# An mLSTM norm without its divisions, a gate maximum taken per tile, and a convolution tap on ScalarE, in a one-core decoder layer

## The chip, the cores and the metric

The kernel runs on one core of one Trainium2 chip. The metric is the device time of one execution in microseconds; the time before is the median of three runs. Engines are named as the profile names them: PE (TensorE matmul), PEld (its weight load), DVE (VectorE), ACT (ScalarE), POOL (GpSimd), SP (SyncE, which here only issues DMAs).

## What is computed

One decoder layer over 1024 tokens of width 1024, in float32. The reference, cut to the parts that the change touches:

```
h = rms_norm(x);  proj = h @ w_in;  u, vm, z, ipre, fpre, qa, ka, va = split(proj)
c = silu(causal_short_conv(u, conv_w, conv_b))            # 4 taps, per channel
# mLSTM, 4 heads x 128, chunks of 128 tokens, running-max stabiliser
b   = cumsum(log_sigmoid(fpre));   g = b_last - b + logi
m_new = maximum(b_last + m, max(g))                       # carried from chunk to chunk
...
den = sum(s) + inter_w * (q . n_prev)
hm  = num / maximum(abs(den), exp(-m_t))
hm  = rms_norm(hm, mh_norm_g) + skip_m * c;   ym = sigmoid(z) * hm
# beside it: dilated attention, 8 heads x 64 -> ya
x = x + concat(ym, ya) @ w_out
# PEER: per token 8 x 16 of 16384 single-neuron experts
x = x + sum_k gelu(h2 . expert_u[idx_k]) * gate_k * expert_v[idx_k]
```

## The kernel before

The 1024 tokens are eight tiles of 128, in three groups: tiles 0-1, 2-5 and 6-7. For each group in turn the program projects (`channels_in`, `project_gates`, `project_conv`, `project_values`, `project_attention`), runs attention with the mLSTM heads woven in (one mLSTM head-half after every fourth attention step, every second one in the last group), then `queries`: the output projection (`acco`, L564), the residual (L567), the second norm, the query projection (`accq`, L598) and the search for the 16 best keys.

The experts are evaluated in two ways. Tiles 2-5 (the middle group, `DENSE`) go through `dense_experts` (L741): all 16384 experts, as matmuls `pu` (up) and `pv` (down), 3072 of each, in pieces of eight chunks; the gates for them are spread out by one-hot products `pg` (`spread_gates`, L710, with casts and copies on ACT), stored to DRAM as `gate_d`, and read back as `gg`. The buffers of `da` (L762) let nine chunks of `pu` stand before a `gg` is needed. Tiles 0, 1, 6 and 7 go the sparse way: POOL gathers 128 rows of 1024 numbers per indirect DMA (L801, five buffers `gt`), and a consumer takes each: for the up side a DVE product with a sum (L813, 128 per tile), for the down side of tiles 0 and 1 a matmul `pov` (L844, two gathers and four matmuls per step, with a small DVE instruction L836 ahead), for the down side of tiles 6 and 7 a DVE multiply-add (L858).

Nobody writes the order of the instructions by hand: a scheduler simulates the program's time line and writes each engine's list from it. Each engine then works through its list in that order. Sparse work, dense work and the front are mixed in the lists, so a changed instruction can change the place of all that comes after it.

The places that the change touches. `gates` (L355) works on 4 partitions (the heads) and n tiles of tokens: after the cumulative sum `bc` (L368) and `gi = logi - bc` (L369) it takes, tile after tile, a running maximum (a scan, L372) that starts from the state `mst`, and then the next state (L373). `mlstm` ends with the norm: L457 and L458 make the denominator, L459 its reciprocal, L460 and L461 its square times the sum of squares, `rstd` (L159 on DVE, the power -1/2 on POOL at L161), L463 the product of both factors, and L465 scales the head (`hn`); PE then transposes it (`pth`, L468), and DVE adds skip and gate (L471, L472) into `mix`, which `queries` needs. `project_conv` copies the accumulator to `uh` on ACT (L267), writes three carried columns (L266), and applies the first tap with the bias (L270) and three further taps (L273) on DVE.

Of the kernel before, what the change touches and what calls it, by code (L numbers as in the profile page):

```python
# [20 lines left out]
P = 128  # L21
# [22 lines left out]
def hybrid_layer(ctx, tc, x, g1, w_in, w_if, conv_w, conv_b, wq, wk, if_b, mh_g, skip, qn_g, kn_g,  # L44
# [212 lines left out]
    def project_conv(g, th, tl):  # L257

        n = GROUPS[g][1]
        W = n * P  # L260
        with pool("su") as st:
            for blk in range(2):
                accs = by_channel(stream(w_in, blk, th, tl, n, True, "u"), n)
                for h, a in enumerate(accs, 2 * blk):
                    uh = st.tile([P, 3 + W], F32, name="uh", bufs=2)
                    nc.vector.tensor_copy(uh[:, 0:3], halo[:, h])  # L266
                    nc.scalar.copy(uh[:, 3:], a)  # L267
                    nc.vector.tensor_copy(halo[:, h], uh[:, W:W + 3])
                    y = st.tile([P, W], F32, name="cy", bufs=2)
                    nc.vector.tensor_scalar(y, uh[:, 0:W], cw_s[:, h, 0:1], cb_s[:, h:h + 1],  # L270
                                            op0=ALU.mult, op1=ALU.add)
                    for j in range(1, 4):
                        nc.vector.scalar_tensor_tensor(y, uh[:, j:j + W], cw_s[:, h, j:j + 1], y,  # L273
                                                       op0=ALU.mult, op1=ALU.add)
                    nc.scalar.activation(uh[:, 0:W], y, AF.Sigmoid)
                    nc.vector.tensor_tensor(y, y, uh[:, 0:W], op=ALU.mult)
                    c_d[g, h] = dram.tile([P, W], F32, name=f"c{g}{h}")
                    nc.sync.dma_start(c_d[g, h], y)
# [76 lines left out]
    def gates(g, cl, ml, gi, gf):  # L355

        tile0, n = GROUPS[g]
        full = [MH, n, P]
        mr = cl.tile(full, F32, name="mr", bufs=2)
        ab = ml.tile([MH, n * P], F32, name="ab", tag="w2r", bufs=2)  # L360
        nc.vector.scalar_tensor_tensor(ab, gf, -1.0, gf, op0=ALU.mult, op1=ALU.max)
        nc.scalar.activation(ab, ab, AF.Exp, scale=-1.0)
        nc.scalar.activation(ab, ab, AF.Ln, bias=1.0)
        nc.vector.scalar_tensor_tensor(gf, gf, 0.0, ab, op0=ALU.min, op1=ALU.subtract)
        bc = ml.tile(full, F32, name="bc")
        for c in range(n):
            f = gf[:, c * P:(c + 1) * P]
            nc.vector.tensor_tensor_scan(bc[:, c], f, f, 0.0, op0=ALU.add, op1=ALU.bypass)  # L368
        nc.vector.tensor_tensor(gi, gi, bc, op=ALU.subtract)  # L369
        for c in range(n):  # L370
            t = tile0 + c
            nc.vector.tensor_tensor_scan(mr[:, c], gi[:, c], gi[:, c], mst[:, t:t + 1], op0=ALU.max, op1=ALU.max)  # L372
            nc.vector.tensor_tensor(mst[:, t + 1:t + 2], mr[:, c, P - 1:P], bc[:, c, P - 1:P], op=ALU.add)  # L373
        pc = pst.tile([P, 4, n, MH], F32, name="pc", tag="tp")
        for q in range(4):
            row = gi
            if q:
                row = ml.tile(full, F32, name="row", tag="w2r", bufs=2)
            if q == 1:
                nc.vector.tensor_tensor(row, mst[:, tile0:tile0 + n, None].to_broadcast(full), mr,  # L380
                                        op=ALU.subtract)
            elif q == 2:
                nc.vector.scalar_tensor_tensor(row, bc, -1.0, mr, op0=ALU.mult, op1=ALU.subtract)
            elif q == 3:
                nc.vector.tensor_tensor(row, gi, mr[:, :, P - 1:P].to_broadcast(full), op=ALU.subtract)
            for c in range(n):
                nc.tensor.transpose(pc[:, q, c], row[:, c], ident[0:MH, 0:MH])
        wcol = cl.tile([P, n, MH], F32, name="wcol", bufs=2)
        nc.vector.tensor_copy(wcol, pc[:, 0])
        ecol = cl.tile([P, 3, n, MH], F32, name="ecol", bufs=2)  # L390
        nc.scalar.activation(ecol, pc[:, 1:4], AF.Exp)
        pa = pst.tile([P, n, MH], F32, name="pa", tag="tp")
        nc.tensor.matmul(pa, lastsel, ecol[:, 0], start=True, stop=True)
        acol = cl.tile([P, n, MH], F32, name="acol", bufs=2)
        nc.vector.tensor_copy(acol, pa)
        return mr, wcol, ecol, acol

    def mlstm(g, half, h, ml, cols, mix):
# [57 lines left out]
        dn = num[:, :, P]  # L456
        nc.vector.scalar_tensor_tensor(sm[:, 1], dn, -1.0, dn, op0=ALU.mult, op1=ALU.max)  # L457
        nc.vector.tensor_tensor(sm[:, 1], sm[:, 1], ecol[:, 1, :, h], op=ALU.max)  # L458
        nc.vector.reciprocal(sm[:, 2], sm[:, 1])  # L459
        nc.vector.tensor_tensor(sm[:, 3], sm[:, 2], sm[:, 2], op=ALU.mult)  # L460
        nc.vector.tensor_tensor(sm[:, 3], sm[:, 3], sm[:, 0], op=ALU.mult)  # L461
        r = rstd(sm[:, 3], P, HT, ml, "rm")
        nc.vector.tensor_tensor(sm[:, 4], r, sm[:, 2], op=ALU.mult)  # L463
        hn = ml.tile([P, HT, P], F32, name="hn", tag="w2m", bufs=5 if g == 0 else 6)
        nc.vector.tensor_tensor(hn, num[:, :, 0:P], sm[:, 4, :, None].to_broadcast([P, HT, P]), op=ALU.mult)  # L465
        pt = pml.tile([P, HW], F32, name="pth", tag="ml")
# [561 lines left out]
```

## Time and profile before

| what | value |
|---|---|
| median of 3 runs | 3063.17 us (3061.2 to 3078.7) |
| profiled execution, its own time | 3072.45 us |
| its span | 3070.7 us |
| PE busy | 2752.9 us (90%) |
| DVE busy | 2355.9 us (77%) |
| ACT busy | 1231.2 us (40%) |
| POOL busy | 1423.7 us (46%) |
| DMA moved | 891.52 MB, mean 290 GB/s |

Busy is the time in which an engine had an instruction in work. Shares over the whole span mix stages: in the first 1680 us the layer's projections, attention and key search stand beside the sparse gathers of tiles 0 and 1; from there to the end PE does the dense experts while the gathers of tiles 6 and 7 run beside it. The rows below are taken stage by stage for that reason.

### The profile page before, as it was taken

To read this page: it belongs to the slowest core of one execution; us is meant where nothing else is said; L and a number is where in the kernel's file an instruction comes from. 1 tells how busy PE (TensorE), PEld (TensorE's weight loads), DVE (VectorE), ACT (ScalarE), POOL (GpSimd) and SP (SyncE) were. 2 spreads that over 40 slices of the span, in tenths; PEclk is the share of its full clock that TensorE was granted. 3 is DMA by queue.
4 is the path that set the end of the run, shared out by engine and by line. 5 is a ranking of instruction groups with operands and counts; after the bars stand their busy time and mean duration, and the time that the engine had idled before them with its cause. 6 is when DMAs were issued, how large, how long until landed. Compare 5 with 4: busy or idle time off the path is not lost.

```text
span 3070.7 us, 43024 instructions
## 1 busy us (share of the span) xinstructions
PE 2752.9 (90%) x14382; PEld 2174.1 (71%) x14382; DVE 2355.9 (77%) x5611; ACT 1231.2 (40%) x2271; POOL 1423.7 (46%) x1139
## 2 busy tenths in 40 slices
PE   6978757798849999889888999999999999999999
PEld 5868557576637565567655887887888787888787
DVE  4559887679874697758874888888998888898853
ACT  4643323354413323589985222332332232333222
POOL 0100567447673444544553455455555555555510
PEclk9979878587869998899998999999999999999999
DMA  6644789789898898798889999999999999999952
GB/s 196 182 149 125 263 296 338 267 317 312 311 334 294 288 322 291 235 330 297 316 298 310 321 335 319 317 335 327 335 329 356 335 315 336 338 337 317 334 181 76
DMA packets 370900, 891.52 MB, mean 290 GB/s; under 512 B 34120, under 2 KB 135496, under 8 KB 366581
## 3 DMA queue, kind: packets, MB, share of 16 engines
q0 software_dynamic: 147456, 536.94, 49.4%
q1 hardware_dynamic: 209076, 307.78, 30.6%
q10 hardware_dynamic: 14144, 44.05, 3.8%
q8 instruction: 113, 1.85, 0.2%
q14 instruction: 111, 0.90, 0.1%
HBM read 831.97 MB, written 61.38 MB: 291 GB/s over the span
## 4 chain that ended last, share of the span: by engine, by line
PE 31%; DMA 7%; issue 7%; DVE 6%; POOL 4%; ACT 2%; POOLq 0%; DVEq 0%; SPq 0%; ACTq 0%
DMA gg<-gate_d 5%; PE pu L154 5%; PE pu L153 5%; PE pu L155 5%; PE pv L154 5%; PE pv L155 5%; PE pv L153 5%; POOL gt L801 4%; DVE hot L722 1%; PE pg L737 1%; DMA gt<-in_expert_u_dram,idx 1%; ACT gs L738 1%; DMA vr<-in_expert_v_dram 1%; PE pov L844 1%; DVE gt L813 1%
## 5 line engine op out<-in xcount | busy, mean ns | idle before, releaser
L801 POOL DMA_INDIRECT gt<-in_expert_u_dram,idx x512 | 679.0, 1326 | 629.3 <-DVE gt L813 370.8
L813 DVE SCALAR_TENSOR_TENSOR gt<-gt,h2s 128x1024 f32<-128x1024 f32 x512 | 617.5, 1219 | 79.5 <-DMA gt<-in_expert_u_dram,idx 78.8
L801 POOL DMA_INDIRECT gt<-in_expert_v_dram,idx x256 | 342.2, 1337 | 281.5 <-DVE acc L858 237.3
L154 PE MATMUL pv<-vlo,dah 128*128 128x512 f32 x1024 | 402.8, 394 | 14.2 <-DVE vlo L790 14.2
L801 POOL DMA_INDIRECT gt<-in_expert_v_dram,idxt x256 | 270.1, 1055 | 310.6 <-PE pov L844 247.8
L153 PE MATMUL pu<-h2th,uhi 128*128 128x512 f32 x1024 | 406.4, 397 | 1.2 <-ACT da L763 1.2
L155 PE MATMUL pu<-h2th,ulo 128*128 128x512 f32 x1024 | 406.3, 397 | 0.7 <-DVE ulo L758 0.7
L154 PE MATMUL pu<-h2tl,uhi 128*128 128x512 f32 x1024 | 406.5, 397 | 0.0
L155 PE MATMUL pv<-vhi,dal 128*128 128x512 f32 x1024 | 401.0, 392 | 0.0
L788 ACT CAST vhi<-vr 128x512 fp32r<-128x512 f32 x256 | 158.2, 621 | 459.2 <-PE pv L155 411.8
L858 DVE SCALAR_TENSOR_TENSOR acc<-gt,act,acc 128x1024 f32<-128x1024 f32 x256 | 327.8, 1281 | 16.3 <-DMA gt<-in_expert_v_dram,idx 14.0
L153 PE MATMUL pv<-vhi,dah 128*128 128x512 f32 x1024 | 317.6, 394 | 13.9 <-ACT dah L149 11.9
L168 ACT CAST wh<-wr 128x512 fp32r<-128x512 f32 x291 | 178.6, 621 | 292.2 <-DMA wr<-in_w_in_dram 54.8
L170 DVE TENSOR_TENSOR wl<-wr,wh 128x512 fp32r<-128x512 f32 x291 | 199.4, 691 | 79.0 <-ACT wh L168 71.3
L154 PEld LDWEIGHTS pv<-vlo,dah 128*128 128x128 f32 x1024 | 193.3, 189 | 61.2 <-DVE vlo L790 19.1
L153 PEld LDWEIGHTS pv<-vhi,dah 128*128 128x128 f32 x1024 | 193.3, 189 | 59.3 <-ACT dah L149 12.3
L790 DVE TENSOR_TENSOR vlo<-vr,vhi 128x512 fp32r<-128x512 f32 x256 | 175.2, 686 | 76.5 <-ACT vhi L788 74.4
L756 ACT CAST uhi<-ur 128x1024 fp32r<-128x1024 f32 x128 | 134.5, 1051 | 235.7 <-PE pu L154 228.1
L153 PEld LDWEIGHTS pu<-h2th,uhi 128*128 128x128 f32 x1024 | 192.7, 188 | 49.8 <-issue 1.7
L154 PEld LDWEIGHTS pu<-h2tl,uhi 128*128 128x128 f32 x1024 | 192.8, 188 | 47.6 <-issue 2.5
L155 PEld LDWEIGHTS pu<-h2th,ulo 128*128 128x128 f32 x1024 | 192.8, 188 | 46.8 <-DVE ulo L758 1.3
L155 PEld LDWEIGHTS pv<-vhi,dal 128*128 128x128 f32 x1024 | 193.6, 189 | 42.1
(280 smaller groups left out, 5727.2 us busy)
## 6 DMA issues: line engine op xcount, KB each, us to landing
ur<-in_expert_ut_dram SPq DMA_DIRECT2D x128, 512.0 KB
vr<-in_expert_v_dram SPq DMA_DIRECT2D x256, 256.0 KB
wr<-in_w_in_dram SPq DMA_DIRECT2D x144, 256.0 KB
gate_d<-gs ACTq DMA_DIRECT2D x32, 1024.0 KB
gg<-gate_d SPq DMA_DIRECT2D x16, 2048.0 KB
wr<-in_w_query_dram SPq DMA_DIRECT2D x96, 256.0 KB
wr<-in_w_out_dram SPq DMA_DIRECT2D x48, 256.0 KB
gt<-in_expert_u_dram,idx POOLq DMA_INDIRECT x512
```

The costliest lines, as they stand in the source:

```text
L153: nc.tensor.matmul(ps, lh, rh, start=first, stop=False)
L154: nc.tensor.matmul(ps, lh, rl, start=False, stop=False)
L155: nc.tensor.matmul(ps, ll, rh, start=False, stop=last)
L168: nc.scalar.copy(wh, wr)
L170: nc.vector.tensor_tensor(wl, wr, wh.bitcast(F32), op=ALU.subtract)
L722: nc.vector.tensor_tensor(o, ids[:, side, None, c0:c0 + half].to_broadcast(full), key128, op=ALU.is_equal)
L756: nc.scalar.copy(uh, ur)
L788: nc.scalar.copy(vh, vr)
L790: nc.vector.tensor_tensor(vl, vr, vh.bitcast(F32), op=ALU.subtract)
L801: nc.gpsimd.indirect_dma_start(out=gt, out_offset=None, in_=table, in_offset=bass.IndirectOffsetOnAxis(ap=idx[:, j:j + 1], axis=0))
L813: nc.vector.scalar_tensor_tensor(gt, gt, 1.0, h2, op0=ALU.mult, op1=ALU.mult, accum_out=pr[:, j:j + 1])
L858: nc.vector.scalar_tensor_tensor(acc, gt, COEF[t][:, j:j + 1], acc, op0=ALU.mult, op1=ALU.add)
```

## The change

Three edits. The norm of an mLSTM head is computed from num and den without forming 1/den: with s the sum of squares and d the denominator, (s/128 + EPS d^2)^(-1/2) takes the place of (1/d) (s/(128 d^2) + EPS)^(-1/2). Five DVE instructions and one on POOL become two and one. In `gates` the state of all tiles comes from one maximum over the tokens and one scan over the tiles, ahead of the scans that give `mr`; the eight small additions go. The first tap of the convolution moves from DVE to ACT.

```
 project_conv
-  nc.vector.tensor_scalar(y, uh[:, 0:W], cw_s[:, h, 0:1], cb_s[:, h:h + 1],
-                          op0=ALU.mult, op1=ALU.add)
+  nc.scalar.activation(y, uh[:, 0:W], AF.Identity, scale=cw_s[:, h, 0:1], bias=cb_s[:, h:h + 1])
 gates
+  top = ml.tile([MH, n], F32, name="top")
+  nc.vector.tensor_reduce(top, gi, AX.X, ALU.max)
+  nc.vector.tensor_tensor_scan(mst[:, tile0 + 1:tile0 + n + 1], top, bc[:, :, P - 1],
+                               mst[:, tile0:tile0 + 1], op0=ALU.max, op1=ALU.add)
   for c in range(n):
       t = tile0 + c
       nc.vector.tensor_tensor_scan(mr[:, c], gi[:, c], gi[:, c], mst[:, t:t + 1], op0=ALU.max, op1=ALU.max)
-      nc.vector.tensor_tensor(mst[:, t + 1:t + 2], mr[:, c, P - 1:P], bc[:, c, P - 1:P], op=ALU.add)
 mlstm
-  nc.vector.reciprocal(sm[:, 2], sm[:, 1])
-  nc.vector.tensor_tensor(sm[:, 3], sm[:, 2], sm[:, 2], op=ALU.mult)
-  nc.vector.tensor_tensor(sm[:, 3], sm[:, 3], sm[:, 0], op=ALU.mult)
-  r = rstd(sm[:, 3], P, HT, ml, "rm")
-  nc.vector.tensor_tensor(sm[:, 4], r, sm[:, 2], op=ALU.mult)
+  nc.vector.scalar_tensor_tensor(sm[:, 2], sm[:, 1], EPS, sm[:, 1], op0=ALU.mult, op1=ALU.mult)
+  nc.vector.scalar_tensor_tensor(sm[:, 3], sm[:, 0], 1.0 / P, sm[:, 2], op0=ALU.mult, op1=ALU.add)
+  nc.gpsimd.tensor_tensor(sm[:, 4], sm[:, 3], mhalf.to_broadcast([P, HT]), op=ALU.pow)
```

Since the scheduler writes the lists anew, the edits move far more than themselves. Three places follow. Lines of the changed kernel behind `gates` have numbers two or three higher: L813 is L815 there, L465 is L467, L468 is L470, L844 is L846.

The first is DVE's list at the norm of the last mLSTM head of the middle group, at the end of that group's attention. Before:

```order
L457 SCALAR_TENSOR_TENSOR sm<-num 128x2
L813 SCALAR_TENSOR_TENSOR gt,pr_s<-gt,h2s 128x1024
L458 TENSOR_TENSOR sm<-sm,ecol 128x2
L813 SCALAR_TENSOR_TENSOR gt,pr_s<-gt,h2s 128x1024
L459 RECIPROCAL sm<-sm 128x2
L813 SCALAR_TENSOR_TENSOR gt,pr_s<-gt,h2s 128x1024
L460 TENSOR_TENSOR sm<-sm 128x2
L461 TENSOR_TENSOR sm<-sm 128x2
L813 SCALAR_TENSOR_TENSOR gt,pr_s<-gt,h2s 128x1024
L159 TENSOR_SCALAR rm<-sm 128x2
L813 SCALAR_TENSOR_TENSOR gt,pr_s<-gt,h2s 128x1024 x2
L463 TENSOR_TENSOR sm<-rmo,sm 128x2
```

In the changed kernel, the same head:

```order
L460 SCALAR_TENSOR_TENSOR sm<-num 128x2
L815 SCALAR_TENSOR_TENSOR gt,pr_s<-gt,h2s 128x1024
L461 TENSOR_TENSOR sm<-sm,ecol 128x2
L815 SCALAR_TENSOR_TENSOR gt,pr_s<-gt,h2s 128x1024
L463 SCALAR_TENSOR_TENSOR sm<-sm 128x2
L815 SCALAR_TENSOR_TENSOR gt,pr_s<-gt,h2s 128x1024
L464 SCALAR_TENSOR_TENSOR sm<-sm 128x2
L815 SCALAR_TENSOR_TENSOR gt,pr_s<-gt,h2s 128x1024 x2
L467 TENSOR_TENSOR hn<-num,sm 128x256
```

The list puts gather products between the small steps of the norm; six of them stood inside the chain, and five stand there now.

The second is PE's list where the last but one mLSTM head of the middle group is transposed (`pth`) and the last one begins (`pq` to `pS`); `pp`, `po` are attention's, `acco` is the output projection. Before:

```order
L468 MATMUL pth<-ident,hn 128x128 x2
L416 MATMUL pq<-cT,wqk 128x256 x2
L422 MATMUL pk<-wqk,cT 128x128 x2
L428 MATMUL pd<-mr,negsel 128x256
L429 MATMUL pd<-mask,ident 128x256
L192 MATMUL acco<-wh,mixh 128x256
L192 MATMUL acco<-wl,mixh 128x256
L192 MATMUL acco<-wh,mixh 128x256
L192 MATMUL acco<-wl,mixh 128x256
L436 MATMUL pS<-mq,mk 128x128 x2
```

In the changed kernel:

```order
L470 MATMUL pth<-ident,hn 128x128 x2
L419 MATMUL pq<-cT,wqk 128x256
L528 MATMUL pp<-ident,ss 128x128 x4
L419 MATMUL pq<-cT,wqk 128x256
L425 MATMUL pk<-wqk,cT 128x128 x2
L532 MATMUL po<-vp,pb 128x64 x4
L528 MATMUL pp<-ident,ss 128x128 x2
L192 MATMUL acco<-wh,mixh 128x256
L192 MATMUL acco<-wl,mixh 128x256
L192 MATMUL acco<-wh,mixh 128x256
L192 MATMUL acco<-wl,mixh 128x256
```

Before, two heads came after attention's last block; now only the last one does, and the one ahead of it ends while attention still has work.

The third is PE's list at the first down matmuls of the dense experts (`pv`). Before:

```order
L155 MATMUL pu<-h2th,ulo 128x512
L153 MATMUL pv<-vhi,dah 128x512 x4
L154 MATMUL pv<-vlo,dah 128x512 x4
L155 MATMUL pv<-vhi,dal 128x512 x4
L153 MATMUL pv<-vhi,dah 128x512 x4
```

In the changed kernel:

```order
L155 MATMUL pu<-h2th,ulo 128x512
L153 MATMUL pv<-vhi,dah 128x512 x4
L846 MATMUL pov<-gt,wv 32x512 x4
L154 MATMUL pv<-vlo,dah 128x512 x4
L155 MATMUL pv<-vhi,dal 128x512 x4
```

All 512 `pov` stood ahead of the first `pv` before; now 460 do, and 52 (13 steps, 26 gathers) come behind it.

## Rows read from the trace of the kernel before

**Rows 1.** The page: span, and PE's busy time with its share.
```profile
span 3070.7 us, 43024 instructions
PE 2752.9 (90%) x14382; PEld 2174.1 (71%) x14382; DVE 2355.9 (77%) x5611; ACT 1231.2 (40%) x2271; POOL 1423.7 (46%) x1139
```
**Rows 2.** Busy time by window: from:to, length, engines (records), granted clock, DMA share, GB/s.
```profile
300.00:560.00 260.00, 171.64 (x993) 149.85 (x992) 213.73 (x472) 74.89 (x117) 157.25 (x116) 0.81 0.86 300
560.00:840.00 280.00, 248.17 (x1339) 193.51 (x1339) 230.81 (x569) 133.16 (x283) 167.85 (x122) 0.80 0.85 299
840.00:860.00 20.00, 14.92 (x71) 12.67 (x70) 18.21 (x37) 7.31 (x18) 16.26 (x11) 0.67 0.78 252
860.00:880.00 20.00, 1.35 (x4) 0.82 (x4) 12.19 (x29) 0.40 (x2) 10.15 (x10) 0.50 1.02 387
880.00:900.00 20.00, 9.35 (x39) 7.63 (x38) 16.56 (x38) 3.96 (x12) 15.99 (x12) 0.67 0.93 336
900.00:910.00 10.00, 1.74 (x7) 1.35 (x7) 8.71 (x21) 0.88 (x2) 8.26 (x8) 0.50 0.87 289
910.00:1290.00 380.00, 363.32 (x2117) 230.94 (x2117) 267.48 (x1337) 133.33 (x269) 168.85 (x162) 0.94 0.84 287
1290.00:1560.00 270.00, 225.89 (x1714) 178.33 (x1714) 211.59 (x784) 245.80 (x498) 140.03 (x132) 0.97 0.88 311
...
1680.00:2940.00 1260.00, 1243.80 (x5343) 1006.64 (x5343) 1083.49 (x1449) 378.09 (x570) 668.18 (x503) 0.99 0.94 329
2940.00:3064.00 124.00, 123.52 (x539) 100.77 (x537) 46.68 (x67) 32.35 (x50) 0.00 (x0) 1.00 0.31 92
```
**Rows 3.** PE's waits: waiting line and releaser, total us, times, longest.
```profile
PE pth L468 <- DVE hn L465: 33.8, 2, 19.3
...
PE pov L844 <- DMA gt<-in_expert_v_dram,idxt: 13.7, 9, 2.9
...
PE pc L387 <- DVE row L380: 12.0, 1, 12.0
PE pv L153 <- ACT dah L149: 11.9, 1, 11.9
```
**Rows 4.** PE's time line: start, us, instruction, idle time before it with its releaser.
```profile
878.65 0.66 PE L468 MATMUL pth<-ident,hn 128*128 128x128 f32 x2 [19.26 <-DVE hn L465]
...
905.49 0.69 PE L468 MATMUL pth<-ident,hn 128*128 128x128 f32 x2 [14.54 <-DVE hn L465]
```
**Rows 5.** DVE's time line between attention's last output and the first residual.
```profile
848.36 0.68 DVE L538 TENSOR_TENSOR ya<-po,den 128x512 f32<-128x512 f32 x1
...
867.57 0.15 DVE L457 SCALAR_TENSOR_TENSOR sm<-num 128x2 f32<-128x2 f32 x1
...
868.98 1.23 DVE L813 SCALAR_TENSOR_TENSOR gt<-gt,h2s 128x1024 f32<-128x1024 f32 x1 [1.25 <-DMA gt<-in_expert_u_dram,idx]
...
878.08 0.42 DVE L465 TENSOR_TENSOR hn<-num,sm 128x256 f32<-128x256 f32 x1
...
920.00 0.75 DVE L567 TENSOR_TENSOR x<-x,acco 128x256 f32<-128x256 f32 x2 [0.78 <-PE acco L192]
```
**Rows 6.** Single lines, minimum/median/maximum ns of one, first and last start.
```profile
L459 DVE RECIPROCAL sm<-sm x16: 148/160/166, 86.8 to 1265.0; 128x2 f32<-128x2 f32 x16
...
L270 DVE TENSOR_SCALAR cy<-uh,cw_s,cb_s x12: 393/408/547, 50.3 to 735.9; 128x256 f32<-128x256 f32 x8, 128x512 f32<-128x512 f32 x4
...
L373 DVE TENSOR_TENSOR mst<-mr,bc x8: 141/143/148, 45.4 to 698.6; 4x1 f32<-4x1 f32 x8
...
L320 DVE TENSOR_REDUCE ssq<-sq x16: 676/680/687, 96.9 to 808.1; 128x8 f32<-128x512 f32 x16
...
L250 ACT ACTIVATE gi<-pif,ifb_s x3: 461/465/677, 31.6 to 677.6; 4x256 f32<-4x256 f32 x2, 4x512 f32<-4x512 f32 x1
```
**Rows 7.** Costliest groups: count, busy us, mean ns, idle before it and what ended it.
```profile
L801 POOL DMA_INDIRECT gt<-in_expert_v_dram,idxt x256 | 270.1, 1055 | 310.6 <-PE pov L844 247.8 <-issue 35.4 <-DVE gt L813 6.1
```

**Rows 8.** The `pov` matmuls (L844) alone, by window, with columns as in rows 2.
```profile
1290.00:1560.00 270.00, 41.12 (x304) 5.98 (x304) 0.97 0.88 311
```

## The prediction, made before the changed kernel was run

> **What bounds the kernel now.** I read four views in this order: busy time by stage, PE's waits, DVE's time line at the longest of them, and the single lines that the edits touch. PE is busy 90% of the span [rows 1], but the stages differ [rows 2]. From 1680 to 2940 us PE is busy 98.7% of the time at a granted clock of 0.99, with the DMA share at 0.94. From 2940 on, with the DMA share down to 0.31, PE completes 539 records in 124 us (4.35 per us) against 5343 in 1260 us (4.24 per us). So the dense experts run at PE's own pace, loaded DMA or not, and the kernel ends when their last matmul does. What can move the end is PE's idle time before 1680 us. It lies in four stretches: 88 us of 260 between 300 and 560, 32 of 280 between 560 and 840, 42.6 of 70 between 840 and 910, 44 of 270 between 1290 and 1560; from 910 to 1290 only 17 of 380 are left.
>
> The longest wait is the one that this change edits: the transposed head `pth` waits 33.8 us for `hn` in two waits [rows 3], 19.26 us up to 878.65 and 14.54 up to 905.49 [rows 4]. The reader is to see in DVE's time line why [rows 5]: the norm's first step starts at 867.57 and `hn` at 878.08, 10.5 us for eight instructions of some 0.16 us each [rows 6] and one on POOL. Between them stand gather products of 1.23 us, and those wait for their gather (1.25 us at 868.98). Each small step costs about one gather's arrival. There the clock is granted at 0.50, the 1.2 GHz level, and the DMA moves 387 GB/s [rows 2]: nearly all that runs is the gathers.
>
> **The direct edits.** Norm, 16 calls (a head and two tiles each): five DVE instructions go, two come, at about 0.16 us [rows 6]: 16 x 3 x 0.16 = 7.7 us of DVE time less. The POOL power stays. First tap: 8 x 0.408 + 4 x 0.547 = 5.5 us leave DVE [rows 6]; ACT takes 8 x 0.465 + 4 x 0.677 = 6.4 us, priced by the same function on as many columns [rows 6] (the Identity of L250, on 4 partitions and read from PSUM; from nothing, where ACT waits anyway, to double). ACT is busy 29% to 48% of 300 to 840 us [rows 2], where eight of the twelve run; behind them on ACT stand the weight casts, which now also wait for the carried columns of L266, a DVE copy that stood ahead of L270 anyway. Gates: eight instructions of 0.143 us go (1.1 us), three maxima come, 0.68 us for 512 columns (the reduction of L320 [rows 6]) and half for 256, 1.4 us together, and three scans over two to four numbers at 0.15 us, 0.45 us. That is 0.7 us more DVE time. PE's wait of 12.0 us for the gate rows [rows 3] stays: in either DVE list the same number of gather products, five, stands between `gi` and the row it waits for. Together DVE loses 12.5 us of work, and most of it was beside other work. On the path I count the norms of the first group, which no gather product interrupts: 4 heads x 3 x 0.16 = 2 us, between 0 and 2.
>
> **The moved work.** This is the larger part.
>
> (a) The end of the middle group's attention. From attention's last output (848.36) to the first residual (920.00) are 71.6 us [rows 5]; DVE's list has 40 gather products in it, so 1.79 us each. In the new list there are 21, because one of the two mLSTM heads that came behind attention now ends inside it (the second order place). 21 x 1.79 = 37.6, 34.0 us less. That head's DVE work, about 4.5 us, now stands ahead of 848, but so do three gather products fewer, 3 x 1.23 = 3.7 us. I take -33 us. Bounds: -19.3, if only one wait of `pth` goes [rows 4], and -42.6, if PE has no idle time left between 840 and 910.
>
> (b) Before it. At the same place in the projections of the last group (807 us), the new list has 7 gather products fewer behind it, of which (a) used 3. DVE is busy 82% of 300 to 840 us [rows 2] and PE waits for it often; 4 x 1.23 = 4.9 us, and I take -4, between 0 and -8.6 (all seven).
>
> (c) The start of the dense experts. PE stood 11.9 us before the first `pv` [rows 3], until gates went to DRAM and came back. Between the last `pg` and the first `pv` PE had 71 `pu` to do; it now has 143, 33 us at the pace of 4.24 per us. I take -6, between -12 and 0, since nine chunks (216 `pu`) is all that the buffers hold, and the new list stops exactly there.
>
> (d) What is given back. 52 `pov` matmuls (13 steps) and 48 `pu` move from ahead of the first `pv` to behind it: 13 x 1.08 = 14 us (41.12 us of PE for 304 records, eight to a step, so 38 steps [rows 8]) and 48 / 4.24 = 11 us. They leave a stage where PE had 16% idle and ACT was busy 91% [rows 2], so there they were partly free; behind, PE has no room. +10, between 0 (PE set that stage) and +25 (ACT set it alone).
>
> From 910 to 1290 PE is busy 96% of the time, so a shift at 910 is carried on; I count nothing there. The gathers that leave the front are done later: at the same dense step the sparse work is about 17 gathers behind where it was, some 40 us at 1260 us for the 512 gathers of tiles 6 and 7. They ended by 2940 with 124 us to spare [rows 2], so that delay stays hidden; without this room it would cost those 40 us.
>
> **Sum.** -2 -33 -4 -6 +10 = -35 us. Made against the profiled execution's own 3072.45 us (span 3070.7) that is 3037; that execution stands 9.3 us, 0.3%, above the median of the runs, so for a median I say 3063.2 - 35 = **3028 us**. All bounds together give -2 -42.6 -8.6 -12 + 0 = -65 and 0 -19.3 + 0 + 0 + 25 = +6, or 2998 to 3069.
>
> **Rivals.** *The deferred gathers are paid for later.* At the tail the DMA did 387 GB/s while PE stood still [rows 2]; that was useful work. The 19 gathers that leave it move 128 x 1024 x 4 bytes each, 10 MB, and at the 329 GB/s of the dense stage 30 us. If the transfers set the pace wherever they go, the -33 comes back: 3063 - 5 = 3058. For it: the DMA share is 0.84 to 0.94 in every later stage. Against it: PE's pace does not change when the share falls to 0.31, and 124 us x 237 GB/s = 29 MB of room lie at the end. The Trainium skill (DMA: Bandwidth & Descriptors, section Bandwidth) states about 358 GB/s as the HBM limit of a core and would make these stages, at 300 to 329, nearly full; by that figure 10 MB would cost an estimated 28 us. The row of 387 GB/s speaks against taking it as the limit here. Chance 0.2.
>
> *The new order buys nothing.* The head that moved into attention delays attention's own DVE work by as much as it saves, and only the direct edits and half of (c) remain: 3063 - 8 = 3055. For it: DVE is the engine that attention and mLSTM share there, 82% busy. Against it: the number of gather products ahead of each step falls, not only their place among themselves. Chance 0.12.
>
> *The late gathers stop PE (slower).* The 13 `pov` steps behind the first `pv` stand among 293 PE matmuls, 69 us at 4.24 per us, so 5.3 us a step. From 1290 to 1560 a step took 7.1 us (38 in 270 us [rows 8]). If its two gathers cannot come faster than that, PE, which works its list in order, stands 13 x 1.8 = 23 us, and if the same slow gathers keep the tail as it was while (d) is given back all the same, the time is 3063 + 23 + 10 = 3096. It decides from 5.3 us a step on. For it: the gate transfers run at just that time. Against it: in those stages the gathers waited 247.8 us for PE's `pov` [rows 7] while PE waited 13.7 us for them [rows 3], so PE's list set the 7.1 us. Chance 0.10.
>
> **How the numbers follow.** The forecast has the remaining 0.58. About 1% (30.6 us) is what a measurement of this kernel can tell from no change. Of the forecast's 0.58, spread by its bounds around 3028, I put 0.46 below 3032.5 and 0.12 above; the first two rivals lie within 1%, 0.32; of the third, half lies above 3094. So faster 0.46, within 1% 0.49, slower 0.05. The range runs from the forecast's low bound, 2998, to 3070, which takes in its high bound and the first two rivals and leaves out the third.
>
> **What would show it.** In the changed kernel's profile `pth` should wait for `hn` once, not twice, at the end of the middle group's attention, 10 to 15 us; the time from attention's last output to the first residual should be near 38 us; the first residual some 37 us earlier, near 883; the first `pv` should wait less than 12 us; the last gather product should end at 2940 or before, with the dense stage at about 4.24 records per us; and PE's waits of `pov` for gathers should stay near 14 us. It is wrong if the residual comes early but the first `pv` does not (the second rival or the first), if `pov` waits tens of us behind the first `pv` (the third), or if the list's shorter tail still takes 60 us or more.

## The result and the profile after

The changed kernel takes 3030.52 us (median of 6 runs, 3023.63 to 3036.69), the kernel before 3072.36 (6 runs, 3061.2 to 3079.27): a ratio of 0.9865, 95% interval 0.984 to 0.9889. The forecast was 3028. The profiled executions took 3025.4 and 3072.45 us, 47 us apart.

The page of the changed kernel, to set beside [rows 1]: PE was busy 17 us less.

```profile
span 3023.6 us, 42958 instructions
PE 2735.5 (90%) x14382; PEld 2157.6 (71%) x14382; DVE 2350.9 (78%) x5552; ACT 1231.9 (41%) x2279; POOL 1414.7 (47%) x1139
```

Busy time by window of the changed kernel, columns as in [rows 2]. The first two rows reach to attention's last output of the middle group, the third is the tail up to the first residual; the rest are the key search, the gate products, and the dense experts.

```profile
300.00:560.00 260.00, 183.79 (x1020) 156.57 (x1021) 209.23 (x443) 82.77 (x134) 153.44 (x115) 0.81 0.85 300
560.00:826.00 266.00, 234.52 (x1372) 187.15 (x1371) 234.09 (x566) 135.05 (x293) 162.68 (x124) 0.87 0.91 317
825.80:863.00 37.20, 14.53 (x81) 12.46 (x79) 26.34 (x58) 5.26 (x13) 23.89 (x20) 0.63 0.97 357
863.00:1210.00 347.00, 330.14 (x1933) 211.15 (x1931) 266.11 (x1310) 125.20 (x259) 161.33 (x151) 0.96 0.85 294
1210.00:1515.00 305.00, 257.95 (x1900) 201.25 (x1900) 243.69 (x842) 279.51 (x559) 160.57 (x151) 0.93 0.87 310
1600.00:2250.00 650.00, 635.96 (x2764) 504.02 (x2763) 518.98 (x710) 186.31 (x280) 343.92 (x260) 0.99 0.93 323
2900.00:3018.00 118.00, 114.36 (x491) 92.89 (x489) 62.48 (x79) 29.69 (x46) 13.35 (x10) 0.99 0.40 137
```

PE still idles in the front and hardly in the dense stage: 2764 records in 650 us are 4.25 per us, as before. Next, PE's waits over the whole span, and PE's time line at the longest wait for a head; they answer to [rows 3, 4].

```profile
PE pth L470 <- DVE hn L467: 20.1, 4, 17.5
PE sc L511 <- DMA kp<-kT: 15.3, 1, 15.3
PE pv L154 <- DVE vlo L792: 15.0, 8, 4.0
PE pov L846 <- DMA gt<-in_expert_v_dram,idxt: 12.2, 11, 3.0
PE pv L153 <- ACT vhi L790: 9.8, 5, 4.5
PE pc L390 <- DVE row L383: 9.8, 2, 9.3
```
```profile
846.37 0.69 PE L470 MATMUL pth<-ident,hn 128*128 128x128 f32 x2 [17.54 <-DVE hn L467]
```

One long wait of `pth` is left where there were two, and the first `pv`'s 11.9 us for `dah` is gone. DVE's time line answers to [rows 5]: attention's last output, the last head's norm from its first step to `hn`, the first residual.

```profile
825.76 0.68 DVE L540 TENSOR_TENSOR ya<-po,den 128x512 f32<-128x512 f32 x1
...
837.08 0.16 DVE L460 SCALAR_TENSOR_TENSOR sm<-num 128x2 f32<-128x2 f32 x1
837.52 1.23 DVE L815 SCALAR_TENSOR_TENSOR gt<-gt,h2s 128x1024 f32<-128x1024 f32 x1 [0.28 <-DMA gt<-in_expert_u_dram,idx]
838.67 0.08 DVE L815 DVE_READ_ACCUMULATOR gt<-gt,h2s 128x1 f32 x1
838.67 0.16 DVE L461 TENSOR_TENSOR sm<-sm,ecol 128x2 f32<-128x2 f32 x1
...
845.89 0.42 DVE L467 TENSOR_TENSOR hn<-num,sm 128x256 f32<-128x256 f32 x1
...
862.96 0.75 DVE L569 TENSOR_TENSOR x<-x,acco 128x256 f32<-128x256 f32 x2 [0.75 <-PE acco L192]
```

The norm still takes 8.8 us from its first step to `hn`, with four small steps on DVE, since a gather product stands behind each. The tail is 37.2 us where it was 71.6, and the residual comes 57 us sooner. Followed to the end (first starts): attention's last output -22.6 us, first residual -57.0, first `pv` -84.5 (1679.7 to 1595.2), the middle `pu` -52.8 (2304.3 to 2251.6), the last instruction -47. So the front won 57 us, the stretch from there to the first `pv` another 27 (much of it work that moved behind that mark), and 37 were given back in the dense stage. These are two single profiles; how far such marks move between profiles of one list is shown in the last section. Both sides of the 37 us are seen in the windows between the first `pv`, the middle `pu` and the end, first of the kernel before, then of the changed one:

```profile
1679.70:2304.30 624.60, 616.55 (x2640) 498.97 (x2641) 537.81 (x723) 189.64 (x287) 327.71 (x248) 0.99 0.94 327
2304.30:3065.80 761.50, 751.07 (x3241) 608.75 (x3239) 593.34 (x794) 221.11 (x332) 340.47 (x256) 1.00 0.84 292
```
```profile
1595.20:2251.60 656.40, 642.36 (x2794) 508.36 (x2793) 525.38 (x720) 188.86 (x283) 347.70 (x261) 0.99 0.93 322
2251.60:3018.70 767.10, 753.90 (x3241) 610.60 (x3239) 614.22 (x811) 221.32 (x333) 360.61 (x273) 0.99 0.86 302
```

Up to the middle `pu` PE has 154 records more behind the first `pv` (but for the window's edges 52 `pov` matmuls, two records each, and 48 `pu`): 25.8 us more of busy time, and 6.0 of idle. In the second half the work is the same 3241 records.

### The profile page after: what moved, and what is told of

It is laid out like the page before. It is cut to its first block, busy times and chain, and to the rows that moved or that the text cites. A ratio compares the mean times of both kernels' runs of the same rounds, so it can differ in the third digit from the quotient of the medians.

```text
span 3023.6 us, 42958 instructions
## 1 busy us (share of the span) xinstructions
PE 2735.5 (90%) x14382; PEld 2157.6 (71%) x14382; DVE 2350.9 (78%) x5552; ACT 1231.9 (41%) x2279; POOL 1414.7 (47%) x1139
## 4 chain that ended last, share of the span: by engine, by line
PE 48%; DMA 13%; issue 13%; DVE 12%; POOL 7%; ACT 6%; SPq 1%; POOLq 0%; DVEq 0%; ACTq 0%
POOL gt L803 7%; DMA gg<-gate_d 5%; PE pu L155 5%; PE pu L154 4%; PE pu L153 4%; PE pv L154 4%; PE pv L153 4%; PE pv L155 4%; PE accq L192 4%; PE pov L846 3%; PE acco L192 3%; DMA gt<-in_expert_u_dram,idx 2%; DVE gt L815 2%; DMA wr<-in_w_in_dram 2%; DMA gt<-in_expert_v_dram,idxt 2%
## 5 line engine op out<-in xcount | busy, mean ns | idle before, releaser
L803 POOL DMA_INDIRECT gt<-in_expert_u_dram,idx x512 | 665.2, 1299 | 630.9 <-DVE gt L815 400.1
L815 DVE SCALAR_TENSOR_TENSOR gt<-gt,h2s 128x1024 f32<-128x1024 f32 x512 | 617.6, 1219 | 71.3 <-DMA gt<-in_expert_u_dram,idx 69.5
L860 DVE SCALAR_TENSOR_TENSOR acc<-gt,act,acc 128x1024 f32<-128x1024 f32 x256 | 327.8, 1280 | 10.9 <-DMA gt<-in_expert_v_dram,idx 8.5
L153 PE MATMUL pv<-vhi,dah 128*128 128x512 f32 x1024 | 324.1, 395 | 9.8 <-ACT vhi L790 9.8
L758 ACT CAST uhi<-ur 128x1024 fp32r<-128x1024 f32 x128 | 134.5, 1051 | 262.2 <-PE pu L154 261.8
```

Of the source, the lines that this page charges most:

```text
L153: nc.tensor.matmul(ps, lh, rh, start=first, stop=False)
L758: nc.scalar.copy(uh, ur)
L803: nc.gpsimd.indirect_dma_start(out=gt, out_offset=None, in_=table, in_offset=bass.IndirectOffsetOnAxis(ap=idx[:, j:j + 1], axis=0))
L815: nc.vector.scalar_tensor_tensor(gt, gt, 1.0, h2, op0=ALU.mult, op1=ALU.mult, accum_out=pr[:, j:j + 1])
L860: nc.vector.scalar_tensor_tensor(acc, gt, COEF[t][:, j:j + 1], acc, op0=ALU.mult, op1=ALU.add)
```

## The experiments

Two theories stood against each other. **A**: the gain comes of the list. Fewer gathers' consumers stand ahead of the front's work on DVE, so the front, and with it the dense experts, come sooner. **B**: the gain is the DVE work that was removed. Besides, C, that each edit brings its own share, and the prediction's rivals. The table has all kernels. "Gathers ahead" are counted in the program's order on DVE (one for each up-side product and each down-side multiply-add, two for each `pov` step), ahead of the middle group's first residual and of the 65th weight split `ulo` of the dense experts (L758, called "dense tile 4's first" in some expectations). Tail and residual are from each one's profiled execution, in us. Each ratio is to runs of the kernel before on the same chip, whose median there was 3067 to 3081 us, so ratios compare and medians do not.

| kernel | gathers ahead of residual / `ulo` | tail | residual at | median us | ratio to before | interval |
|---|---|---|---|---|---|---|
| before | 261 / 762 | 71.6 | 920.0 | - | 1 | - |
| full change | 239 / 745 | 37.2 | 863.0 | 3030.52 | 0.9865 | 0.984 to 0.9889 |
| the same, again | 239 / 745 | 36.1 | 870.9 | 3040.74 | 0.9898 | 0.9856 to 0.9939 |
| norm only | 241 / 741 | 35.5 | 877.0 | 3006.9 | 0.9785 | 0.9721 to 0.9848 |
| the same, again | 241 / 741 | 33.4 | 869.6 | 3006.04 | 0.9802 | 0.9762 to 0.9842 |
| convolution only | 245 / 751 | 49.5 | 878.2 | 3042.62 | 0.989 | 0.9832 to 0.9948 |
| gates only | 266 / 762 | 75.1 | 936.1 | 3074.11 | 1.0016 | 0.9991 to 1.0041 |
| norm and convolution | 248 / 750 | 25.0 | 872.3 | 3025.04 | 0.9845 | 0.9794 to 0.9897 |
| norm and gates | 243 / 742 | 35.4 | 880.1 | 3010.81 | 0.9797 | 0.9745 to 0.9849 |
| norm, three idle steps | 260 / 759 | 64.8 | 910.3 | 3065.9 | 0.9985 | 0.9953 to 1.0018 |
| before, one idle step | 258 / 754 | 76.7 | 903.0 | 3046.91 | 0.9926 | 0.9893 to 0.9959 |
| before, heads every third | 261 / 762 | 60.0 | 927.5 | 3071.85 | 0.9978 | 0.9945 to 1.0011 |
| before, four buffers | 233 / 718 | 60.3 | 910.0 | 3136.03 | 1.0186 | 1.0125 to 1.0248 |
| full change, tile 7's down side left out | 239 / 745 | 35.1 | 855.5 | 3012.74 | 0.983 | 0.9763 to 0.9896 |

**The parts alone and in pairs.** Each takes over hunks of the change's diff and leaves the rest as before. The norm only:

```
-        nc.vector.reciprocal(sm[:, 2], sm[:, 1])
...
+        nc.vector.scalar_tensor_tensor(sm[:, 2], sm[:, 1], EPS, sm[:, 1], op0=ALU.mult, op1=ALU.mult)
+        nc.vector.scalar_tensor_tensor(sm[:, 3], sm[:, 0], 1.0 / P, sm[:, 2], op0=ALU.mult, op1=ALU.add)
+        nc.gpsimd.tensor_tensor(sm[:, 4], sm[:, 3], mhalf.to_broadcast([P, HT]), op=ALU.pow)
```

> Only the norm is changed, gates and first tap are as before. In the instruction lists this leaves 20 gathers fewer ahead of the first residual of the middle group (226 of them ahead of the last norm there instead of 246), and 21 fewer ahead of the 65th weight split of the dense experts. Theory A (the front ends earlier by the gathers that no longer stand ahead of it, about 2.4 us each at the dense stage, as 17 of them answer to the 42 us that the whole change brought): 21 x 2.4 = 50 us less, ratio 0.984. Theory B (only the DVE instructions removed and those on the exposed norms count, 7.7 us of DVE time and 0.5 us per exposed chain): 0 to 10 us less, ratio 0.997 to 1.0. Theory C (the three edits each bring about a third): 14 us less, ratio 0.995.

The convolution only:

```
-  nc.vector.tensor_scalar(y, uh[:, 0:W], cw_s[:, h, 0:1], cb_s[:, h:h + 1],
...
+  nc.scalar.activation(y, uh[:, 0:W], AF.Identity, scale=cw_s[:, h, 0:1], bias=cb_s[:, h:h + 1])
```

> Only the first convolution tap is on ScalarE, norm and gates are as before. The lists hold 16 gathers fewer ahead of the first residual and 11 fewer ahead of the 65th weight split. Theory A: 11 x 2.4 = 26 us less, ratio 0.991. Theory B: 5.5 us of DVE time less, mostly hidden, 0 to 5 us, ratio 0.998 to 1.0. Theory C: 14 us less, ratio 0.995.

The gates only:

```
+        nc.vector.tensor_reduce(top, gi, AX.X, ALU.max)
...
-            nc.vector.tensor_tensor(mst[:, t + 1:t + 2], mr[:, c, P - 1:P], bc[:, c, P - 1:P], op=ALU.add)
```

> Only the gates' maximum is changed. The lists hold 5 gathers more ahead of the first residual and none more or fewer ahead of the 65th weight split. Theory A: 0 us, ratio 1.0 (at most +10 us). Theory B: DVE gets 0.7 us more work, ratio 1.0. Theory C: 14 us less, ratio 0.995.

The first and the second of these diffs together:

> Norm and first tap are changed, the gates are as before. The lists hold 13 gathers fewer ahead of the first residual and 12 fewer ahead of the 65th weight split, so fewer than with the norm alone. Theory A: 12 x 2.4 = 29 us less, ratio 0.991, slower than the norm alone by some 20 us although it holds less DVE work. Theory B: 0 to 15 us less and no slower than the norm alone. Theory C: 28 us less and faster than the norm alone by 14 us.

The first and the third:

> The norm without its divisions and the gates' maximum with its scan, without the convolution's first tap on ACT. 18 gather products fewer than before ahead of the first residual and 20 fewer ahead of dense tile 4's first weight split. Theory A (2.4 us for each gather fewer ahead): 48 us less, 3019 us, ratio 0.984. Theory C (each edit brings its own part, as measured alone: norm -60 us by the medians, gates +7): 3010 to 3015 us. If the convolution's tap on ACT costs something beside the norm (the full change and norm with convolution were both slower than norm alone, by 18 to 24 us), then norm with gates is as fast as norm alone, 3005 to 3012 us.

The norm alone gains 60 us by medians and 66 by the ratio, the convolution 25 and 34, the gates nothing; they don't add up, so C fails: the full change gains less than its largest part. B fails too: norm and convolution remove more DVE work than the norm does and gain no more. A had the order right, but not every size: it expected 0.984 for the norm and 0.991 for norm and convolution, and the second of these lies above the measured interval. By `ulo`, the gains of these kernels, as (1 - ratio) of their time of before, are 2.9 to 4.0 us per gather fewer ahead, where A had 2.4; the full change gets 1.8 to 2.4. The pairs point at the convolution as the part that costs something beside the norm: norm and gates (0.9797) is as fast as the norm alone, norm and convolution (0.9845) is not by its median, though its interval overlaps the norm's.

**Idle steps: the same list lever without the edits.** To the norm-only kernel three steps that change nothing are added in the norm's chain; to the kernel before, one.

```
+        nc.vector.tensor_scalar(sm[:, 1], sm[:, 1], 1.0, None, op0=ALU.mult)     # three times, or once
         nc.vector.scalar_tensor_tensor(sm[:, 2], sm[:, 1], EPS, sm[:, 1], ...)   # in the kernel before: the reciprocal
```

> The norm without its divisions (and nothing else of the change), with three idle steps put back into its chain: three times sm = 1.0 x sm on 128x2 numbers, ahead of the new steps, 16 calls x 3 x 0.16 us = 7.7 us of DVE work, the same work that the norm edit took away. In the program's order 41 gather products then stand between attention's last output and the first residual (24 in the norm alone, 44 before), 260 ahead of the first residual (241 and 261), 759 ahead of dense tile 4's first weight split (741 and 762). Theory A (number of gather products ahead): the tail is 62 to 72 us again, the first residual at 910 to 922 us, the end within 10 us of before, 3057 to 3070 us; nearly all of the norm's gain of 60 us is gone for 7.7 us of work. Theory B (DVE work removed is the gain): 7.7 us of work bring back 7.7 us, 3012 to 3018 us. The rival that the division itself was the cost: 3007 to 3015 us.

> The kernel before with one idle step more in the norm (sm = 1.0 x sm, 128x2 numbers, 16 calls of 0.16 us, 2.6 us of DVE work added). In the program's order 7 gather products fewer stand ahead of attention's last output (210 for 217), but 4 more behind it, so 258 for 261 ahead of the first residual, and 754 for 762 ahead of dense tile 4's first weight split. Theory A: attention's last output 10 to 17 us sooner (near 835 us, where before has 848.4), a longer tail (75 to 80 us), the first residual 0 to 10 us sooner, the end 8 to 25 us sooner although the kernel does more: 3040 to 3060 us. Theory B: 3 us later, 3066 to 3070 us.

These two decide between A and B. The single lines of the norm-only kernel with idle steps (columns as in [rows 6]) show what was added, 16 x 3 x 0.166 = 8.0 us, and DVE's time line its tail from attention's last output to the first residual:

```profile
L461 DVE TENSOR_SCALAR sm<-sm x16: 149/166/170, 84.9 to 1253.0; 128x2 f32<-128x2 f32 x16
```
```profile
845.51 0.69 DVE L541 TENSOR_TENSOR ya<-po,den 128x512 f32<-128x512 f32 x1 [0.62 <-PE po L533]
...
910.34 0.75 DVE L570 TENSOR_TENSOR x<-x,acco 128x256 f32<-128x256 f32 x2 [0.78 <-PE acco L193]
```

Eight microseconds of idle work take the gain back: the tail is 64.8 us again, two waits of `pth` are back, and the ratio is 0.9985, with 1 in its interval:

```profile
868.54 0.69 PE L471 MATMUL pth<-ident,hn 128*128 128x128 f32 x2 [19.35 <-DVE hn L468]
...
895.20 0.69 PE L471 MATMUL pth<-ident,hn 128*128 128x128 f32 x2 [12.84 <-DVE hn L468]
```

The division itself is not in this kernel, so it was not the cost. The other way round, the kernel before with 2.6 us of idle work more:

```profile
826.29 0.69 DVE L540 TENSOR_TENSOR ya<-po,den 128x512 f32<-128x512 f32 x1 [2.86 <-PE po L532]
...
902.98 0.75 DVE L569 TENSOR_TENSOR x<-x,acco 128x256 f32<-128x256 f32 x2 [0.76 <-PE acco L193]
```

It is 0.74% faster, 1 - 0.9926, some 23 us, for 8 gathers fewer ahead of `ulo`. Attention's last output comes 22 us sooner (A said 10 to 17), the tail is 5 us longer, as the list has it, and the residual 17 us sooner (A said 0 to 10). Work added made it faster; only the list explains that.

**The place of the heads alone.** In the kernel before, the heads are woven after every third attention step in the middle group:

```
-  chain(*(mlstm_half(1, half, mx.tiles, cols, mix) for half in range(2))), 4))
+  chain(*(mlstm_half(1, half, mx.tiles, cols, mix) for half in range(2))), 3))
```

> The kernel before, with the mLSTM heads woven into the middle group's attention after every third step in place of every fourth. The count of gather products ahead of the first residual stays 261, and ahead of dense tile 4's first weight split 762; two heads' transposes stand behind the attention's last transposes in place of three. Theory A (the count of gathers ahead decides): no change within 0.5%, 3060 to 3075 us, and a first residual near 915 us. The rival that the place of the last heads decides (one head less behind the attention, worth some 15 to 20 us: the pth wait of 19.3 us in the tail goes): 3047 to 3052 us.

The tail shrinks by 11.6 us, but attention's last output comes 19.1 us later (867.5 for 848.4), and the time stays: a head that moves into attention without fewer gathers ahead pays there what it saves behind.

**Fewer gathers ahead by fewer buffers.** In the kernel before:

```
-        gt = sp.tile([P, D], F32, name="gt", bufs=5)
+        gt = sp.tile([P, D], F32, name="gt", bufs=4)
```

> The kernel before, with four gather buffers (gt) in place of five and nothing else. The program's order then has 28 gather products fewer ahead of the attention's first residual (233 where before has 261) and 44 fewer ahead of dense tile 4's first weight split (718 for 762), with the norm, the convolution and the gates as they were. Theory A (the front ends earlier because gather products of 2.4 us each no longer stand ahead of it; the edits' own work is small): first residual near 860 to 875 us where before has 920, tail behind the attention's last output under 55 us where before has 71.6; the end comes sooner too, by 20 to 60 us, less what four buffers cost the sparse stream (each gather has one buffer less of lead), so 3010 to 3060 us. Theory B (the gain is DVE work removed): nothing is removed here, so no gain, 3067 or later by what the missing buffer costs. The rival that deferred gathers are paid for later: residual sooner, end at 3067 or later.

Here A's forecast failed: 44 gathers fewer ahead of `ulo`, and 1.9% slower. The residual comes 10 us sooner (A said 45 to 60) and the first `pv` 14 us; the loss lies behind that. There PE idles 55 us where before has 18, and is busy 51 us more, of which 24.5 are 184 `pov` records that this list has behind the first `pv`. DVE's waits for gathers over the whole span, of this kernel and then of the kernel before (up side, then down side):

```profile
DVE gt L813 <- DMA gt<-in_expert_u_dram,idx: 147.6, 135, 5.9
DVE acc L858 <- DMA gt<-in_expert_v_dram,idx: 59.2, 53, 3.0
```
```profile
DVE gt L813 <- DMA gt<-in_expert_u_dram,idx: 78.8, 81, 4.1
DVE acc L858 <- DMA gt<-in_expert_v_dram,idx: 14.0, 16, 2.0
```

DVE waits 114 us longer, and the products of the dense experts' `da` with the gates stand in its list behind the waiting gathers. ACT, which casts `da` and the weights in turn, waits for them; from 1700 us on, of this kernel and then of the kernel before:

```profile
ACT dah L149 <- DVE da L769: 461.7, 108, 14.0
```
```profile
ACT dah L149 <- DVE da L769: 256.3, 87, 9.6
```

PE's wait of `pv` for `vhi`, a cast of ACT, grows from 2.0 to 41.5 us. That this chain makes all of the added idle time is argued, not shown.

So the count of gathers ahead orders the kernels only while each gather has the same lead. Over the table's rows with five buffers it does so roughly: a straight line through them has 2.5 us of residual for each gather ahead (an estimate from the table, with every row within 14 us of the line). For the time and the count ahead of `ulo` it is 2.9 us for each, without the row that leaves work out, and the full change's two rows lie 7 and 17 us above that line. The scheduler wrote each list from its own time line, and ahead of `ulo` only tile 6's down-side products differ in number, so the count may mark how early the front ends as much as cause it. The idle steps show that the order of the list makes the gain; that this count is what matters in the order is not shown. A holds for the change in that sense, not as a rule for buffers.

**Are the deferred gathers paid for?** The changed kernel without the expert down side of tile 7, whose output is x2:

```
+            if t == 7:
+                acc = sp.tile([P, D], F32, name="acc", tag="acc", bufs=1)
+                nc.sync.dma_start(acc, x2_d[t])
+                nc.sync.dma_start(out[t * P:(t + 1) * P], acc)
+            else:
                 (experts_out_pe if t in ON_PE else experts_out)(t)
```

> The changed kernel without the expert down side of tile 7: x2 of that tile is copied to the output instead, so 128 gathers of the last tile's down rows and their products are left out. It tests whether gathers that the change pushes back are paid for at the end. If the dense passes set the end and the gathers lie beside them (forecast), leaving 128 of them out shortens the time by no more than the last tile's closing steps and what pov took from PE: 128 products of 0.1 to 0.2 us on PE beside dense ones, up to 25 us, more likely 0 to 15. If the sparse stream of gathers is a second bound behind the dense passes, 128 gathers at the 2.4 to 3.5 us that they take apiece come off, some 100 to 300 us for the part that overhung: over 50 us is its mark.

It takes 3012.74 us, a ratio of 0.983 (0.9763 to 0.9896), against 0.9865 and 0.9898 for the full change; the intervals overlap, and the gap is 11 to 21 us, 0.08 to 0.16 us for each of the 128 gathers. (Their products run on DVE; `pov`, of which the expectation speaks, is the way of tiles 0 and 1.) The same window late in the dense stage, without those gathers and then with them:

```profile
2620.00:2920.00 300.00, 300.00 (x1303) 244.43 (x1302) 122.21 (x168) 90.05 (x134) 0.00 (x0) 1.00 0.38 117
```
```profile
2620.00:2920.00 300.00, 296.61 (x1275) 240.04 (x1274) 258.22 (x281) 88.69 (x133) 159.51 (x121) 0.99 0.95 331
```

121 gathers in 300 us, with the DMA share at 0.95, cost PE 28 records of 1303, 6.5 us: 0.05 us for each gather. By either figure that is far below the 2.5 to 3 us for each that stands ahead of the front, so the deferral pays.

**Norm alone against the full change, on one chip.** Both as above, without a further edit.

> The norm without its divisions alone, again, beside the full change on the same chip. If norm alone is the faster of the two (3006.9 us, ratio 0.9785 to before, against 0.9865 for the full change, measured apart), then its ratio is 0.976 to 0.983 here and the full change's 0.983 to 0.990, some 20 us apart. If the gap came of the two occasions, the two agree within 8 us.

> The changed kernel itself, again, on the same chip as the norm alone: ratio to before 0.984 to 0.989, 3020 to 3035 us, and 10 to 25 us behind the norm alone if the convolution's first tap on ACT costs something beside the norm; even with it if not.

Norm alone is the faster, by 34.7 us of the medians, and the intervals do not meet. It beats both kernels. In the profiled executions the residual comes at the same time (869.6 and 870.9 us), and the first `pv` 16 us sooner. The windows behind the first `pv`, up to the middle `pu` and on to the end, of the norm alone and then of the full change:

```profile
1601.50:2241.50 640.00, 629.68 (x2737) 497.76 (x2738) 518.55 (x716) 189.05 (x287) 333.27 (x255) 0.99 0.93 324
2241.50:3000.00 758.50, 749.66 (x3241) 607.43 (x3239) 617.71 (x815) 220.26 (x333) 364.58 (x276) 1.00 0.88 309
```
```profile
1617.50:2274.90 657.40, 643.68 (x2794) 509.49 (x2793) 525.65 (x720) 189.03 (x283) 347.18 (x261) 0.99 0.92 322
2274.90:3047.30 772.40, 755.61 (x3241) 611.89 (x3239) 614.14 (x811) 221.37 (x333) 360.78 (x272) 0.99 0.86 300
```

Of the 47 us between these two profiles (34.7 by medians: the full change's profiled run was the slowest of its six), 14.0 are the busy time of 57 records more behind the first `pv`: the norm alone still has 264 `pu` ahead of it, the full change 216, though the full change's first `pv` comes no sooner. Norm and gates, as fast as the norm alone, has 238 there, so this count alone does not order the kernels. Another 8 us are idle time in the second half, 16.8 us against 8.8, where PE waits for the down weights; why their casts come later there stays open. The stretch from the residual to the first `pv` is 15 us longer as well. In the first profile of the full change it was not, with the same list, and there the granted clock differs. The rows are the full change's first profile, its second, and the kernel without tile 7's down side, whose lists are the same up to 2335 us:

```profile
863.00:1595.20 732.20, 663.88 (x4218) 467.51 (x4217) 550.28 (x2228) 452.81 (x897) 350.75 (x325) 0.94 0.86 302
870.90:1617.50 746.60, 678.78 (x4217) 476.99 (x4217) 550.28 (x2228) 452.99 (x897) 350.41 (x325) 0.92 0.84 297
855.50:1577.90 722.40, 648.74 (x4217) 458.29 (x4216) 553.75 (x2227) 452.49 (x897) 351.29 (x325) 0.97 0.87 307
```

The same matmuls kept PE busy 648.7, 663.9 and 678.8 us at a mean granted clock of 0.97, 0.94 and 0.92, and the 14.9 us between the first and the second profile of the full change are as much as the stretch is longer (14.4). What lowered the clock in one run and not in the other stays open.

## Why the prediction was right, and where not

The profiled times are 47 us apart, the forecast was 35; by medians it was 42, and 33 in the repetition. That the median of 3030.5 lies so near the 3028 is partly luck: with six runs the kernel before stands at 3072.4 and not at 3063.2, and the gain was 7 us larger than forecast. In the profiles two misses work against each other as well, more gained in the front and more given back behind it. The residual came 57 us sooner, in the second profile 49, where 37 were expected. The chances gave 0.46 to a gain of more than 1% and 0.49 to less than that either way; both occasions lie above 1%, the second only just.

- **What bounds** was right: the dense stage kept its pace, and the time came from PE's idle stretches in the front. The mark of 2940 us held in the first profile, where the last gather's multiply-add ends at 2935.8; in the second it ends at 2964.5, still 88 us before the end.
- **(a), the tail**, -33, was right in mechanism and size: 71.6 to 37.2 us (forecast 37.6), one `pth` wait left (17.5 us, a little over the 10 to 15 expected). Its two counts, 40 and 21, take in four small `pov` instructions each (36 and 17 products); the difference of 19 is untouched.
- **(b), before the tail**, -4 with a bound of -8.6, is the term that was mis-sized: with the direct edits' -2 it makes -6, and -22.6 were measured. The windows from the start to the gates' `gi` and from there to attention's last output, before and after, tell what was missed:

```profile
0.00:372.30 372.30, 301.57 (x1936) 263.89 (x1936) 254.16 (x910) 174.59 (x365) 47.97 (x45) 0.91 0.58 180
372.30:848.40 476.10, 369.05 (x2056) 301.73 (x2057) 384.51 (x859) 179.69 (x362) 299.47 (x220) 0.78 0.87 306
```
```profile
0.00:364.60 364.60, 296.68 (x1936) 259.66 (x1936) 249.71 (x893) 175.25 (x367) 46.85 (x44) 0.93 0.59 182
364.60:825.80 461.20, 364.18 (x2120) 298.97 (x2121) 385.01 (x850) 188.43 (x387) 284.86 (x219) 0.83 0.90 316
```

  DVE's busy time fell by 4.0 us in both together, about what the terms priced. The rest, 18.6 us, is DVE's idle time. Between `gi` and attention's last output its waits for gathers fell from 35.0 to 27.2 us, those for attention's scores (`ss` for `sc`) from 19.6 to 11.3. I priced instructions that move, at their duration, and left out that on an engine that works through its list every wait moves with them. No run takes these waits apart, and the granted clock differs too, 0.78 before and 0.83 after in the second stretch, so what each of them is worth is not shown. Part of it is chance: in the second profile of the same program this output comes at 834.8, so -13.6, and in the kernel without tile 7's down side, whose list is the same up to there, at 820.4, so -28.0; all three are beyond the bound.
- **(c)**, -6, was right in mechanism and too small: the whole wait of 11.9 us is gone. With 143 `pu` between the last `pg` and the first `pv` there is none; the kernels with 50 to 71 wait 10.9 to 12.4 us, those with 79 to 143 at most 4.2. **(d)**, the work given back, was priced at 14 + 11 = 25 us and measured as 25.8 of PE's busy time; the 104 `pov` records behind the first `pv` took 13.85 us. But PE also idles 6.0 us more in that stretch, and the last one takes 5.6 us longer. From the residual to the end the net is +10, where (c) and (d) had +4; in the second profile, whose clock was lower in part of it, it is +31.
- **The rivals.** *Paid for later* fell by the kernel without 128 of the gathers: 0.05 us each in the window, at most 0.16 by the whole time, so some 20 deferred gathers cost a few us and not 30. The Trainium skill's figure of about 358 GB/s (DMA: Bandwidth & Descriptors, Bandwidth), which spoke for it, is, by the same section, the share with both cores of a pair at work; the row of 381 GB/s below agrees that one core alone passes it. *The new order buys nothing* is what the heads' place alone does, not what the change does. *Late gathers stop PE*: `pov` waited 12.2 us in all, 13.7 before, and 3.4 behind 1200 us.

What the forecast did not say is that the edits work against each other: 0.8 to 1.0% of the time lies between the norm alone and all three. It looked at the list of the whole change only; a list for each edit shows 264 `pu` ahead of the first `pv` for the norm alone and 216 for all three.

## What to carry to other kernels

Where one engine works through a list that mixes urgent small steps with bulk work, count the bulk items that stand ahead of each urgent step, before and after: here an item cost about 3 us in the front and 0.05 us where the matmuls cover it, and three idle steps of 0.17 us in a chain moved nineteen of them. Check that the bulk stream keeps its buffers before taking the count as a rule: with one buffer less it failed. Price such a move with the waits that travel with it, not with instruction times alone. And time the parts of a change separately: the scheduler answers to each, and the best of them may be one part alone. Profile each program more than once before a mark in one trace is put down to an edit.

## What the hardware showed besides

- Each gather product with its sum is two instructions on DVE, 1.23 us and an accumulator read of 0.08 us, as the Trainium skill has it (VectorE: DVE Perf Modes, Two Vector instructions with no wait between them). The read's record begins before the product's ends and reaches only 0.008 us beyond it on average, so the 512 reads of the changed kernel add some 4 us to DVE's busy time.
- With PE almost idle in the tail, the DMA moved 381 GB/s and the mean granted clock was 0.63, so for most of it at the 1.2 GHz level (0.50). Of the 7.63 MB in this window 4.55 are gathers, and the rest are loads that SP issued for the last group; in the window that the prediction read as nearly all gathers (860 to 880 us of the kernel before, 387 GB/s) it is 4.42 of 7.74 MB. The second row is the gathers' queue: packets, MB, share:

```profile
826.00:846.00 20.00, 2.25 (x18) 1.82 (x17) 14.35 (x31) 2.54 (x8) 13.47 (x12) 0.63 1.02 381
...
q0 software_dynamic: 1256, 4.55, 56.7%
```

- The same list's profile differed by 14 us at one instruction of the front (attention's last output at 820.4, 825.8 and 834.8 us) and by 40 us at the first `pv` (1577.9, 1595.2 and 1617.5), and the changed kernel's ratio by 0.3% between two occasions (0.9865 and 0.9898). A term of a few microseconds in such a front is within that.
